# Loading, casting and turning the first two x pairs by row tile in a QKV projection, and casting the second w block by slices

## The chip, the core and the metric

The kernel runs on one core of a Trainium2 chip. The metric is the device time of one execution in microseconds (us); several executions are taken and their median is given. The program's engines are TensorE (PE for its matmuls, PEld for its weight loads), VectorE (DVE), ScalarE (ACT) and GpSimd (POOL); SyncE (SP) issues most of the DMAs, and its instructions run in program order like those of the others.

## The reference

`x` has the shape 16 x 512 x 768, `w_qkv` 768 x 2304, both float32. The output is 3 x 16 x 512 x 768, float32.

```python
qkv = np.matmul(x, w_qkv)
q = qkv[..., :hidden]
k = qkv[..., hidden:2*hidden]
v = qkv[..., 2*hidden:]
return np.stack([q, k, v], axis=0).astype(np.float32)
```

So it is one matrix product of 8192 x 768 by 768 x 2304, whose result is stored in three parts.

## The kernel before, in words

The 8192 rows of x are worked through in 32 pairs `p` of two row tiles of 128 rows. The 2304 columns of w are split into four blocks of 512, named by `q` (left or right half) and `c` (first or second block of that half), and a remainder of 256 columns (`w_rem`). K = 768 is split into six slices `j` of 128. w is loaded in float32 and rounded on the chip: block (0, 0) into `b1[0]` and block (0, 1) into `bt`, both bf16.

From pair 2 on, a half's 2 x 2 blocks are multiplied with seven products in place of eight (a scheme of Strassen's kind). It needs sums and differences of blocks of w (`sum_w`, on DVE, L119) and of x (`sums_x`, `s`), which take the time in which w is still being loaded. Pairs 0 and 1 are therefore multiplied plainly: `block(q, c, w, groups)` (L433) goes over groups of k slices and row tiles, adds into one PSUM bank a row tile, and gives back a list of ACT copies from PSUM (`finish`, L441) that the caller places. Row tiles 0 to 3 are the two of pair 0 and the two of pair 1.

The order of all work is written out by hand (`tc.manual_schedule()`), so each engine runs its instructions in the order in which the program makes them. What stands at the start, L399 to L566, is this:

- DMA issues on SP: pair 0 of x as one DMA (`load_rows`, L161), pair 1 as another, six slices of w block (0, 0) of 256 KB each, two halves of block (0, 1) of 768 KB each (L92), the first two of eight parts of pair 2 (L137, `load_x_rows`), the remainder of w (`str`), the other six parts of pair 2, then the halves of block (1, 0).
- Each DMA has one of eight completion semaphores in turn, and SP issues a DMA only when the one eight places earlier has landed. The trace shows this: the ninth issue comes at 5.01 us, pair 0 having landed at 4.99.
- Pairs 0 and 1 are cast to bf16 (`cast_rows`, half a row tile on DVE, L165, half on ACT, L167), turned by PE transposes (L187), six a row tile, and copied out of PSUM by the same two lines (`turn_rows`).
- PE first runs dummy matmuls on a tile of zeros (`busy`, L418), 11 ahead of the first transposes and 4 between the pairs.
- The slices of block (0, 0) are cast by DVE (`cast_k`, L429). `block(0, 0)` is 24 matmuls of 512 columns (L449). Its order, `singles`, gives pair 0 the first two slices ahead of pair 1.
- The halves of block (0, 1) are cast whole, the first by DVE (L426), the second by ACT (L424). Then come `sum_w(0, 1)` and `sum_w(0, 2)` on DVE, a cast of a half into `b22[0]` on POOL (L502), the four copies out of PSUM of block (0, 0) on ACT, and the casts of the remainder, half on DVE (L505), half on ACT (L506).
- `block(0, 1)` is another 24 matmuls; `rem(0)` and `rem(1)` are 24 of 256 columns (L303).
- Pair 2 is turned by DVE in two steps (`transpose(2, 2)`, L153): the first step needs parts 0 to 3 of its load, the second parts 4 to 7. A part is 96 KB and writes 32 of the 128 partitions. ACT then rounds row tile 0 (`round_row`, L204), copies `rems[0]` out (L317), copies two banks (L441), rounds row tile 1, copies `rems[1]`, and evacuates pair 2's product 1 (`evacuate`, L257).
- PE goes on with pair 2's products 1 and 2 (`do`, L248), its remainder (`rem(2)`, whose second half needs row tile 1), and product 6, which adds into the bank that `evacuate` reads, so it has to come after that.

From there on, products of pair 2 alternate with the plain blocks of the right half, and then the loop over the pairs runs.

Of the kernel before, what the change touches and what calls it, by code (L numbers as in the profile page):

```python
# [10 lines left out]
def kernel(  # L11
# [20 lines left out]
    nc = tc.nc  # L32
    P = 128
# [15 lines left out]
    bf16 = mybir.dt.bfloat16  # L49
    ident = mybir.ActivationFunctionType.Identity  # L50
# [3 lines left out]
    x_flat = x.rearrange("b t h -> (b t) h")  # L54
# [5 lines left out]
    tq_pool = ctx.enter_context(tc.tile_pool(name="tq", bufs=2))  # L60
# [14 lines left out]
    eye = w_pool.tile([P, 176], bf16, name="eye")[:, :P]  # L75
    w_rem = [w_pool.tile([P, KH, REM], bf16, name="w_rem0"), None]

    b1 = [w_pool.tile([P, KT, CB], bf16, name=f"b1_{q}") for q in range(2)]
# [6 lines left out]
    bt = both[:, 1].bitcast(bf16).rearrange("p (j n) -> p j n", j=KT)  # L85
# [4 lines left out]
    def load_w(dst, j0, nj, off, cols):  # L90
        rows = w_qkv.rearrange("(p j) n -> p j n", j=KT)
        nc.sync.dma_start(dst, rows[:, j0:j0 + nj, off:off + cols])  # L92

    stage = {}

    def load_blocks(q, c, nj=KH):
        if q == 0:
            t = tq_pool.tile([P, KT, CB], fp32, name="st0", tag="tq")
            for j in range(0, KT, nj):
                load_w(t[:, j:j + nj], j, nj, Q_OFF[q] + c * CB, CB)  # L100
            stage[q, 0, c], stage[q, 1, c] = t[:, :KH, :], t[:, KH:, :]
        else:
            for h in range(2):
                if c == 0 and h == 0:
                    t = st_first
                else:
                    t = st_pool.tile([P, KH, CB], fp32, name="st1", tag="st")[:]
                load_w(t, h * KH, KH, Q_OFF[q] + c * CB, CB)
                stage[q, h, c] = t

    def sum_w(q, n):
        t1, t2, t3, t4 = ts[q]
        o, in0, in1 = {
            1: (t1, stage[q, 0, 1], stage[q, 0, 0]),
            2: (t2, stage[q, 1, 1], t1),
            3: (t3, stage[q, 1, 1], stage[q, 0, 1]),
            4: (t4, stage[q, 1, 0], t2),
        }[n]
        nc.vector.tensor_tensor(o, in0, in1, op=sub)  # L119

    xin, xf, xb, sr = {}, {}, {}, {}
# [8 lines left out]
    def load_x_rows(p, parts=range(8)):  # L130
        if p not in xin:
            xin[p] = xin_pool.tile([P, 2 * P // G, KC], fp32, name="xin")
        rows = x_flat[p * 2 * P:(p + 1) * 2 * P, :].rearrange("(g b) k -> b g k", b=G)
        for n in parts:
            r, i = divmod(n, 4)
            gs = slice(r * P // G, (r + 1) * P // G)
            nc.sync.dma_start(  # L137
                xin[p][i * G:(i + 1) * G, gs], rows[:, gs, i * KC:(i + 1) * KC]
            )
# [15 lines left out]

    def load_rows(p):
        xin[p] = xin_pool.tile([P, 2, K], fp32, name="xin")
        rows = x_flat[p * 2 * P:(p + 1) * 2 * P, :]  # L160
        nc.sync.dma_start(xin[p][:], rows.rearrange("(r m) k -> m r k", m=P))  # L161

    def copy_halves(dst, src, two):

        nc.vector.tensor_copy(out=dst[0], in_=src[0])  # L165
        if two:
            nc.scalar.activation(dst[1], src[1], ident)  # L167
        else:
            nc.vector.tensor_copy(out=dst[1], in_=src[1])

    xc = {}

    def cast_rows(p, two=True):
        src = xin.pop(p)
        xc[p] = s_pool.tile([P, 2, K], bf16, name="xc", tag="s")
        for r in range(2):
            halves = (slice(0, K // 2), slice(K // 2, K))
            copy_halves([xc[p][:, r, n] for n in halves], [src[:, r, n] for n in halves], two)

    def turn_rows(p, two=True):  # L180
        c = xc.pop(p)
        xb[p] = xb_pool.tile([P, KT, 2 * P], bf16, name="xb", tag="xb")
        for r in range(2):
            cols = c[:, r, :].rearrange("m (p j) -> m j p", j=KT)
            ps = ps_pool.tile([P, KT, P], bf16, name="ps")
            for j in range(KT):
                nc.tensor.transpose(ps[:, j, :], cols[:, j, :], eye)  # L187
            ks = (slice(0, KH), slice(KH, KT))
            copy_halves(
                [xb[p][:, n, r * P:(r + 1) * P] for n in ks], [ps[:, n, :] for n in ks], two  # L190
            )

    def round_x(p):
        xb[p] = xb_pool.tile([P, KT, 2 * P], bf16, name="xb", tag="xb")
# [2 lines left out]
    act, dve = nc.scalar, nc.vector  # L197
# [32 lines left out]
    def quad(p, q, pool=o_pool, tag="o"):  # L230
        u = Quad()
        u.p, u.q = p, q
        u.o = pool.tile([P, 2, 2 * CB], fp32, name="o", tag=tag)
        u.x = u.y = u.z = None
        return u
# [17 lines left out]
    def bank():  # L253
        return ps_pool.tile([P, CB], fp32, name="ps")
# [144 lines left out]
    ND = 2  # L399
    zero = xb_pool.tile([P, CB], bf16, name="zero", tag="xb")  # L400
    nc.vector.memset(zero[:], 0.0)  # L401
    load_rows(0)
    nc.scalar.activation(tiny[:], zero[:, :1], ident)
    make_identity(nc, eye)
    load_rows(1)
    load_blocks(0, 0, 1)
    load_blocks(0, 1)
    st_rem = o_pool.tile([P, KT, REM], fp32, name="str", tag="o")
    load_x_rows(2, range(2))
    load_w(st_rem[:], 0, KT, R_OFF, REM)  # L410
    load_x_rows(2, range(2, 8))
    load_blocks(1, 0)

    def busy(n):

        ps = bank()
        for _ in range(n):
            nc.tensor.matmul(ps[:], zero[:, :P], zero[:], start=True, stop=True)  # L418

    def cast(q, h, c, w, eng):  # L420

        dst = w[:, h * KH:(h + 1) * KH, :]
        if eng is act:
            eng.activation(dst, stage[q, h, c], ident)  # L424
        else:
            eng.tensor_copy(out=dst, in_=stage[q, h, c])  # L426

    def cast_k(j):
        dve.tensor_copy(out=b1[0][:, j, :], in_=stage[0, j // KH, 0][:, j % KH, :])  # L429

    quads = {}

    def block(q, c, w, groups, between={}):  # L433

        ps = {}
        late = []

        def finish(n):
            p, r = divmod(n, 2)
            u = quads[p, q]  # L440
            act.activation(u.o[:, r, c * CB:(c + 1) * CB], ps[n][:], ident)  # L441

        for i, (js, tiles) in enumerate(groups):
            for n in tiles:
                p, r = divmod(n, 2)
                if n not in ps:
                    ps[n] = bank()
                for j in js:
                    nc.tensor.matmul(  # L449
                        ps[n][:], xb[p][:, j, r * P:(r + 1) * P], w[:, j, :],  # L450
                        start=(j == 0), stop=(j == KT - 1), skip_group_check=True,
                    )
                if KT - 1 not in js:
                    continue
                if (p, q) not in quads:
                    quads[p, q] = quad(p, q)
                late.append(lambda n=n: finish(n))
            between.get(i, lambda: None)()
        return late

    def halves(tiles):
        return [(range(h * KH, (h + 1) * KH), tiles) for h in range(2)]
# [18 lines left out]
        round_x(p)  # L481
        sums_x(p)

    singles = [((0, ), (0, 1)), ((1, ), (0, 1)), ((0, 1), (2, 3))]
    singles += [((j, ), range(4)) for j in range(2, KT)]

    busy(11)
    cast_rows(0)
    turn_rows(0)
    busy(4)  # L490
    cast_rows(1)
    cast_k(0)
    cast_k(1)
    turn_rows(1)
    for j in range(2, KT):
        cast_k(j)
    late0 = block(0, 0, b1[0], singles)
    cast(0, 0, 1, bt, dve)
    cast(0, 1, 1, bt, act)
    sum_w(0, 1)  # L500
    sum_w(0, 2)
    nc.gpsimd.tensor_copy(out=b22[0][:], in_=stage[0, 1, 1])  # L502
    for f in late0:
        f()
    dve.tensor_copy(out=w_rem[0][:], in_=st_rem[:, :KH])  # L505
    act.activation(w_rem[1][:], st_rem[:, KH:], ident)  # L506
    late = block(0, 1, bt, halves(range(4)))
    rems = [rem(p) for p in range(2)]
    transpose(2, 2)

# [19 lines left out]
    sum_w(0, 3)  # L530
    sums[3](dve)
    sums[4](dve)

    def cast_j(q, c, w, j):
        act.activation(w[:, j, :], stage[q, j // KH, c][:, j % KH, :], ident)

    u = quad(2, 0)
    do(u, 1)
# [2 lines left out]
    rem2 = rem(2)  # L541
    middle(u)
    cast_j(1, 0, b1[1], 1)
    store2 = []

# [16 lines left out]
    late = block(1, 0, b1[1], slices, {0: rest, 3: end})  # L562
# [65 lines left out]
```

## Time and profile before

| what | value |
|---|---|
| median of 3 executions | 361.02 us (360.87 to 361.2) |
| the profiled execution, its own time | 361.09 us |
| its span, first to last instruction | 359.3 us |
| time around the span | 1.79 us |
| PE busy | 352.2 us, 98% of the span |
| DVE, ACT, POOL busy | 229.0, 186.6, 176.7 us |
| moved by DMA | 108.09 MB, 301 GB/s in the mean |

A line of the timeline reads: start, duration, engine, line of the kernel, operation, what is written and read, shapes, number of instructions merged into it, and in brackets the idle time of the engine just before it and what ended that. Times are counted from the start of the span. A group's duration goes from its first start to its last end, and as matmuls are pipelined, groups overlap. An arrow `<-` in the brackets names the one waited for. Weight loads run beside matmuls.

### The profile page before, as it was taken

The numbers are of one execution on the slowest core, as the hardware profiler recorded it, in microseconds if no ns is written. First come the engines' busy times: TensorE is split into PE (matmuls) and PEld (weight loads), VectorE is DVE, ScalarE is ACT, GpSimd is POOL, SyncE is SP. The second block draws the span as 40 slices with busy tenths as digits, with TensorE's granted clock in tenths as the row PEclk, the third lists the DMA queues.
The fourth block names the chain that finished last, engine by engine and source line by source line (L and its number), as shares of the span: only waits on it lengthen the run. The fifth ranks groups of instructions, "written<-read, shape, count | busy, mean of one in ns | idle before, by whom it ended". The sixth has DMA issues, their size and how long they took to land.

```text
span 359.3 us, 5225 instructions
## 1 busy us (share of the span) xinstructions
PE 352.2 (98%) x1748; PEld 251.8 (70%) x1779; DVE 229.0 (64%) x241; ACT 186.6 (52%) x316; POOL 176.7 (49%) x183
## 2 busy tenths in 40 slices
PE   8999999999999999999999999999999999999995
PEld 3465577777777777777777777777777777777764
DVE  3899776666566675566675556676556676556643
ACT  4489744545444545444445444445444445545443
POOL 0101766436665445665444665444665444665420
PEclk9999999999999999999999999999999999999999
DMA  7999999798999999899999899898999999999767
GB/s 298 359 361 337 317 359 386 234 345 305 277 315 305 291 285 281 288 307 310 292 287 280 290 297 328 282 288 278 293 291 318 294 296 272 281 298 323 290 238 260
DMA packets 81563, 108.09 MB, mean 301 GB/s; under 512 B 4993, under 2 KB 61569, under 8 KB 81537
## 3 DMA queue, kind: packets, MB, share of 16 engines
q1 hardware_dynamic: 67216, 97.14, 82.9%
q10 hardware_dynamic: 14320, 10.62, 9.0%
q8 instruction: 14, 0.23, 0.3%
q14 instruction: 13, 0.10, 0.1%
HBM read 32.24 MB, written 75.50 MB: 300 GB/s over the span
## 4 chain that ended last, share of the span: by engine, by line
PE 97%; ACT 1%; issue 1%; ACTq 0%; DVE 0%
PE ps L248 78%; PE ps L303 11%; PE ps L449 6%; PE ps L418 1%; PE ps L187 1%; ACT o L283 0%; ACTq L358 0%; ACT orem L372 0%; ACT xb L167 0%; ACT xc L167 0%; ACTq L374 0%; DVE xb L165 0%; DVE zero L401 0%; ACTq L372 0%
## 5 line engine op out<-in xcount | busy, mean ns | idle before, releaser
L248 PE MATMUL ps<-t,s 128*128 128x512 f32 x720 | 181.2, 399 | 0.0
L248 PEld LDWEIGHTS ps<-t,s 128*128 128x128 f32 x720 | 135.0, 188 | 30.8
L195 POOL CAST xb<-xf 128x1536 bf16<-128x1536 f32 x28 | 41.0, 1464 | 131.6 <-DVE xf L153 131.6
L280 DVE TENSOR_TENSOR o<-o,ps 128x512 f32<-128x512 f32 x58 | 39.9, 688 | 91.2 <-ACT o L279 91.2
L153 DVE STREAM_TRANSPOSE xf<-xin 128x1536 f32<-128x1536 f32 (+1 forms) x32 | 88.7, 2774 | 1.3 <-DMA xin<-in_x_dram 1.2
L248 PE MATMUL ps<-b,xb 128*128 128x512 bf16 x331 | 85.1, 380 | 1.5
L248 PEld LDWEIGHTS <-xb 128*128 128x128 bf16 x360 | 32.8, 98 | 37.3 <-issue 7.6
L273 ACT ACTIVATE o<-ps 128x512 f32<-128x512 f32 x60 | 36.0, 600 | 44.1 <-PE ps L248 41.4
L279 ACT ACTIVATE o<-ps 128x512 f32<-128x512 f32 x58 | 34.7, 598 | 44.2 <-PE ps L248 44.2
L286 DVE TENSOR_TENSOR o<-o,ps 128x512 f32<-128x512 f32 x60 | 41.2, 687 | 21.4 <-PE ps L248 20.2
L248 PE MATMUL ps<-b,s 128*128 128x512 f32 x180 | 50.4, 389 | 0.0
L283 ACT ACTIVATE o<-ps 128x512 f32<-128x512 f32 x60 | 35.9, 598 | 24.5 <-PE ps L248 21.6
L257 ACT ACTIVATE o<-ps 128x512 f32<-128x512 f32 x60 | 35.9, 598 | 24.4 <-DVE o L286 20.7
L303 PE MATMUL ps<-w_rem,xb 128*128 128x256 bf16 x384 | 47.4, 273 | 0.0
L303 PEld LDWEIGHTS <-xb 128*128 128x128 bf16 x384 | 37.3, 98 | 11.5 <-issue 0.8
L270 DVE TENSOR_TENSOR o<-o,ps 128x512 f32<-128x512 f32 x60 | 37.8, 672 | 2.0 <-ACT o L257 1.3
L248 PEld LDWEIGHTS ps<-b,s 128*128 128x128 f32 x180 | 33.8, 188 | 7.1
L215 POOL TENSOR_TENSOR s<-xf 128x384 fp32r<-128x384 f32 x29 | 30.9, 1065 | 0.0
L216 POOL TENSOR_TENSOR s<-s,xf 128x384 fp32r<-128x384 f32 x29 | 29.5, 1016 | 2.3
L217 POOL TENSOR_TENSOR s<-xf 128x384 fp32r<-128x384 f32 x29 | 29.5, 1017 | 0.0
L219 POOL TENSOR_TENSOR s<-xf,s 128x384 fp32r<-128x384 f32 x29 | 29.5, 1017 | 0.0
L317 ACT ACTIVATE orem<-ps 128x512 f32<-128x512 f32 x31 | 18.5, 597 | 19.6 <-PE ps L303 19.6
(45 smaller groups left out, 119.5 us busy)
## 6 DMA issues: line engine op xcount, KB each, us to landing
out_dram<-o SPq DMA_DIRECT2D x62, 768.0 KB, 5.2
out_dram<-o SPq DMA_DIRECT2D x65, 256.0 KB, 4.1
xin<-in_x_dram SPq DMA_DIRECT2D x62, 192.0 KB, 6.9
xin<-in_x_dram ACTq DMA_DIRECT2D x50, 192.0 KB, 4.4
out_dram<-orem SPq DMA_DIRECT2D x31, 256.0 KB, 5.8
st<-in_w_qkv_dram SPq DMA_DIRECT2D x5, 768.0 KB, 8.0
xin<-in_x_dram SPq DMA_DIRECT2D x2, 768.0 KB, 5.0
st<-in_w_qkv_dram SPq DMA_DIRECT2D x6, 256.0 KB, 6.0
```

Of the source, the lines that this page charges most:

```text
L153: nc.vector.transpose(turned[:, g:g + n], rows[:, g:g + n])
L195: nc.gpsimd.tensor_copy(out=xb[p][:], in_=xf[p][:])
L215: 1: lambda g: g.tensor_tensor(s[:, 1], a21, a22, op=add),
L248: nc.tensor.matmul(ps[:], lhs[j], rhs[j], start=(start and j == 0), stop=(j == KH - 1), skip_group_check=True,)
L257: nc.scalar.activation(u.o[:, 0, :CB], u.x[:], ident)
L270: nc.vector.tensor_tensor(c11, c11, u.z[:], op=add)
L273: nc.scalar.activation(c12, u.x[:], ident)
L279: nc.scalar.activation(c22, u.x[:], ident)
L280: nc.vector.tensor_tensor(c22, c22, u.y[:], op=add)
L283: nc.scalar.activation(c21, u.x[:], ident)
L286: nc.vector.tensor_tensor(c12, c12, u.y[:], op=add)
L303: nc.tensor.matmul(ps, xb[p][:, j, r * P:(r + 1) * P], w_rem[j // KH][:, j % KH, :], start=(j == 0), stop=(j == KT - 1), skip_group_check= ...
```

## The change

Each row tile of pairs 0 and 1 gets a DMA, a cast and a turn of its own. Three row tiles are loaded ahead of w's first block, the fourth ahead of that block's last slice. The dummy matmuls go from 11 and 4 to 8, 2 and 1. Block (0, 0) takes row tiles 0 to 2 slice by slice, and row tile 3, turned ahead of the last slice, comes last with all six slices. The second w block is cast by slices on DVE and ACT instead of by halves, with the PSUM copies of block (0, 0) between them; its product takes the first half by slices. Only one part of pair 2 is loaded ahead of the remainder of w instead of two. The second half of the remainder is cast by POOL instead of ACT, ahead of the cast into `b22[0]`, and `b22[0]` thus waits for the remainder's landing. The bytes that are moved and the products are the same.

```diff
-    def load_rows(p):
...
-        nc.sync.dma_start(xin[p][:], rows.rearrange("(r m) k -> m r k", m=P))
+    def load_row(p, r):
...
+        nc.sync.dma_start(xin[p][:, r], x_flat[row:row + P, :])
...
-    load_rows(0)
+    load_row(0, 0)
     nc.scalar.activation(tiny[:], zero[:, :1], ident)
     make_identity(nc, eye)
-    load_rows(1)
-    load_blocks(0, 0, 1)
+    load_row(0, 1)
+    load_row(1, 0)
+    load_first(range(KT - 1))
+    load_row(1, 1)
+    load_first((KT - 1, ))
     load_blocks(0, 1)
+    load_x_rows(2, (0, ))
     st_rem = o_pool.tile([P, KT, REM], fp32, name="str", tag="o")
-    load_x_rows(2, range(2))
     load_w(st_rem[:], 0, KT, R_OFF, REM)
-    load_x_rows(2, range(2, 8))
+    load_x_rows(2, range(1, 8))
     load_blocks(1, 0)
...
-    singles = [((0, ), (0, 1)), ((1, ), (0, 1)), ((0, 1), (2, 3))]
-    singles += [((j, ), range(4)) for j in range(2, KT)]
-
-    busy(11)
-    cast_rows(0)
-    turn_rows(0)
-    busy(4)
-    cast_rows(1)
-    cast_k(0)
-    cast_k(1)
-    turn_rows(1)
-    for j in range(2, KT):
-        cast_k(j)
-    late0 = block(0, 0, b1[0], singles)
-    cast(0, 0, 1, bt, dve)
-    cast(0, 1, 1, bt, act)
+    three = [((j, ), range(3)) for j in range(KT)] + [(range(KT), (3, ))]
+
+    busy(8)
+    cast_row(0, 0)
+    turn_row(0, 0)
+    busy(2)
+    cast_row(0, 1)
+    cast_row(1, 0)
+    turn_row(0, 1)
+    busy(1)
+    cast_j(0, 0, b1[0], 0, dve)
+    turn_row(1, 0)
+    for j in range(1, KT - 1):
+        cast_j(0, 0, b1[0], j, dve)
+    cast_row(1, 1)
+    cast_j(0, 0, b1[0], KT - 1, dve)
+    late0 = block(0, 0, b1[0], three, {KT - 2: lambda: turn_row(1, 1)})
+    cast_j(0, 1, bt, 0, dve)
+    late0[0]()
+    late0[1]()
+    cast_j(0, 1, bt, 1, act)
+    cast_j(0, 1, bt, 2, dve)
+    late0[2]()
+    late0[3]()
     sum_w(0, 1)
+    cast_j(0, 1, bt, 3, dve)
+    cast_j(0, 1, bt, 4, act)
+    cast_j(0, 1, bt, 5, act)
     sum_w(0, 2)
+    dve.tensor_copy(out=w_rem[0][:], in_=st_rem[:, :KH])
+    nc.gpsimd.tensor_copy(out=w_rem[1][:], in_=st_rem[:, KH:])
     nc.gpsimd.tensor_copy(out=b22[0][:], in_=stage[0, 1, 1])
-    for f in late0:
-        f()
-    dve.tensor_copy(out=w_rem[0][:], in_=st_rem[:, :KH])
-    act.activation(w_rem[1][:], st_rem[:, KH:], ident)
-    late = block(0, 1, bt, halves(range(4)))
+    late = block(
+        0, 1, bt, [((j, ), range(4)) for j in range(KH)] + [(range(KH, KT), range(4))]
+    )
     rems = [rem(p) for p in range(2)]
     transpose(2, 2)
```

`cast_row` and `turn_row` hold the bodies of the loops over `r` of `cast_rows` and `turn_rows`; `cast_j` casts one k slice of a w block on ACT or DVE; `load_first` allocates the stage tile of block (0, 0) and loads the slices asked for. All that follows `transpose(2, 2)` is as before.

More of the change, by code (lines that the diff above doesn't have):

```diff
@@ L94, with load_first, load_blocks @@
     stage = {}
-    def load_blocks(q, c, nj=KH):
+    def load_first(js):
+        if (0, 0, 0) not in stage:
+            t = tq_pool.tile([P, KT, CB], fp32, name="st0", tag="tq")
+            stage[0, 0, 0], stage[0, 1, 0] = t[:, :KH, :], t[:, KH:, :]
+        for j in js:
+            load_w(stage[0, j // KH, 0][:, j % KH:j % KH + 1, :], j, 1, Q_OFF[0], CB)
+    def load_blocks(q, c):
         if q == 0:
             t = tq_pool.tile([P, KT, CB], fp32, name="st0", tag="tq")
-            for j in range(0, KT, nj):
-                load_w(t[:, j:j + nj], j, nj, Q_OFF[q] + c * CB, CB)
+            for j in range(0, KT, KH):
+                load_w(t[:, j:j + KH], j, KH, Q_OFF[q] + c * CB, CB)
             stage[q, 0, c], stage[q, 1, c] = t[:, :KH, :], t[:, KH:, :]
@@ L154, in transpose, with copy_halves @@
         xf[p] = t
-    def load_rows(p):
-        xin[p] = xin_pool.tile([P, 2, K], fp32, name="xin")
-        rows = x_flat[p * 2 * P:(p + 1) * 2 * P, :]
-        nc.sync.dma_start(xin[p][:], rows.rearrange("(r m) k -> m r k", m=P))
-    def copy_halves(dst, src, two):
+    def load_row(p, r):
+        if r == 0:
+            xin[p] = xin_pool.tile([P, 2, K], fp32, name="xin")
+        row = (2 * p + r) * P
+        nc.sync.dma_start(xin[p][:, r], x_flat[row:row + P, :])
+    def copy_halves(dst, src):
@@ L165, in copy_halves @@
         nc.vector.tensor_copy(out=dst[0], in_=src[0])
[L166 to L169, printed above, removed]
+        nc.scalar.activation(dst[1], src[1], ident)
     xc = {}
[L173 to L191, printed above, removed]
+    def cast_row(p, r):
+        if r == 0:
+            xc[p] = s_pool.tile([P, 2, K], bf16, name="xc", tag="s")
+        halves = (slice(0, K // 2), slice(K // 2, K))
+        copy_halves([xc[p][:, r, n] for n in halves], [xin[p][:, r, n] for n in halves])
@@ L193, in round_x, with turn_row @@
+    def turn_row(p, r):
+        if r == 0:
+            xb[p] = xb_pool.tile([P, KT, 2 * P], bf16, name="xb", tag="xb")
+        cols = xc[p][:, r, :].rearrange("m (p j) -> m j p", j=KT)
+        ps = ps_pool.tile([P, KT, P], bf16, name="ps")
+        for j in range(KT):
+            nc.tensor.transpose(ps[:, j, :], cols[:, j, :], eye)
+        ks = (slice(0, KH), slice(KH, KT))
+        copy_halves([xb[p][:, n, r * P:(r + 1) * P] for n in ks], [ps[:, n, :] for n in ks])
     def round_x(p):
@@ L418, in busy, with cast_j @@
             nc.tensor.matmul(ps[:], zero[:, :P], zero[:], start=True, stop=True)
-    def cast(q, h, c, w, eng):
-        dst = w[:, h * KH:(h + 1) * KH, :]
+    def cast_j(q, c, w, j, eng=act):
+        src = stage[q, j // KH, c][:, j % KH, :]
         if eng is act:
-            eng.activation(dst, stage[q, h, c], ident)
+            eng.activation(w[:, j, :], src, ident)
         else:
-            eng.tensor_copy(out=dst, in_=stage[q, h, c])
-    def cast_k(j):
-        dve.tensor_copy(out=b1[0][:, j, :], in_=stage[0, j // KH, 0][:, j % KH, :])
+            eng.tensor_copy(out=w[:, j, :], in_=src)
     quads = {}
@@ L532 @@
     sums[4](dve)
-    def cast_j(q, c, w, j):
-        act.activation(w[:, j, :], stage[q, j // KH, c][:, j % KH, :], ident)
     u = quad(2, 0)
```

## The prediction

> **What bounds the kernel now.** First the totals and the chain that ended last, on the page:
>
> ```profile
> PE 352.2 (98%) x1748; PEld 251.8 (70%) x1779; DVE 229.0 (64%) x241; ACT 186.6 (52%) x316; POOL 176.7 (49%) x183
> ...
> PE 97%; ACT 1%; issue 1%; ACTq 0%; DVE 0%
> ```
>
> PE is the bound nearly everywhere, so a gain at the start reaches the end only if PE stays ahead at every later wait. I therefore read PE's timeline over the first 26 us, where the change lies:
>
> ```profile
> 1.19 4.87 PE L418 MATMUL ps<-zero 128*128 128x512 bf16 x11 [1.19 <-DVE zero L401]
> 5.85 1.44 PE L187 MATMUL ps<-eye,xc 128*128 128x128 bf16 x12
> 7.12 1.03 PE L418 MATMUL ps<-zero 128*128 128x512 bf16 x4
> 8.67 0.95 PE L187 MATMUL ps<-eye,xc 128*128 128x128 bf16 x12 [0.52 <-ACT xc L167]
> 9.46 5.34 PE L449 MATMUL ps<-b,xb 128*128 128x512 bf16 x23
> 14.64 5.34 PE L449 MATMUL ps<-both,xb 128*128 128x512 bf16 x24
> 19.82 2.78 PE L303 MATMUL ps<-w_rem,xb 128*128 128x256 bf16 x24
> 22.66 1.24 PE L248 MATMUL ps<-b,xb 128*128 128x512 bf16 x5
> 23.74 1.47 PE L303 MATMUL ps<-w_rem,xb 128*128 128x256 bf16 x12
> 25.03 1.66 PE L248 MATMUL ps<-t,s 128*128 128x512 f32 x6
> ```
>
> PE idles once (0.52 us) and starts the first real matmul at 9.46. From there the groups follow without a gap. At 25.03 comes pair 2's product 6, which has to follow ACT's `evacuate` (L257). So ACT's timeline is next:
>
> ```profile
> 20.97 0.84 ACT L204 ACTIVATE xb<-xf 128x768 bf16<-128x768 f32 x1 [0.78 <-DVE xf L153]
> 21.72 0.58 ACT L317 ACTIVATE orem<-ps 128x512 f32<-128x512 f32 x1
> 22.20 1.08 ACT L441 ACTIVATE o<-ps 128x512 f32<-128x512 f32 x2
> 23.15 0.85 ACT L204 ACTIVATE xb<-xf 128x768 bf16<-128x768 f32 x1
> 23.88 0.61 ACT L317 ACTIVATE orem<-ps 128x512 f32<-128x512 f32 x1
> 24.36 0.62 ACT L257 ACTIVATE o<-ps 128x512 f32<-128x512 f32 x1
> ```
>
> ACT waits for DVE's transpose of pair 2, then runs six steps back to back until 24.98, and PE arrives at 25.03: ACT and PE meet there, with no slack on either side. What DVE waited for:
>
> ```profile
> 18.37 0.56 DVE L505 CAST w_rem<-str 128x768 bf16<-128x768 f32 x1
> 19.37 3.25 DVE L153 STREAM_TRANSPOSE xf<-xin 128x768 f32<-128x768 f32 x2 [0.44 <-DMA xin<-in_x_dram]
> ```
>
> DVE was free at 18.93 and waited 0.44 us for part 3 of pair 2, which the trace lands at 19.25. **A second chain thus ends at 25.03**: landing of part 3, transpose, six ACT steps, product 6. The change shortens PE's own way to 25.03, and touches the other chain only through the order of DMAs and POOL's casts.
>
> **Part by part.**
>
> *Arrival of x and w.* In the trace pair 0 (768 KB) lands at 4.99 and pair 1 at 6.89, 1.90 us later; a row tile is half, 0.95. The w slices land at 7.53, 8.22, 8.86, 9.46, 10.11 and 10.81, the halves of block (0, 1) at 12.72 and 14.95. With the new order I estimate row tiles at 4.04, 5.0 and 5.95, the first five slices 0.95 earlier (6.6 to 9.15), row tile 3 at 10.1, the last slice at 10.8 as before. SP has two more DMAs at about 0.45 us each (the two pairs' issues take 0.95 together). The ninth and tenth now wait for row tiles 0 and 1, and are issued at about 5.05 for bytes that move after 9.1: hidden.
>
> *PE until block (0, 0).* Dummies start every 0.43 us at first (eleven in 4.66) and 12 transposes take 1.27, 0.106 each; later they take 0.79, and a block matmul (14.64 - 9.46) / 24 = 0.216. Eight dummies end at 4.6. Row tile 0's casts (DVE 0.36, ACT 0.52) end at 4.58: six transposes until 5.3, two dummies until 6.15. The copies from PSUM start some 0.25 after the last transpose's start slot, and in the trace ACT's (0.49) starts only after DVE's (0.36) in all four pairs, so ACT ends row tile 0's at 6.4 and casts row tile 1 until 6.85. PE idles some 0.7 us there. Transposes, one dummy, transposes of row tile 2 until 7.9; casts of slices at 0.42 on DVE let block (0, 0) start at 8.3 instead of 9.46. Three matmuls a slice (0.65) keep step with the slices (0.64). Six more transposes (0.35) lie inside the block, and 24 matmuls take 5.2: it ends at 13.85, against 14.64. **PE's lead is 0.8 us**, or 0.3 if row tile 3's copies hold up the last slice by half a microsecond.
>
> *Block (0, 1).* Its first slice is cast on DVE from 12.74 (landing 12.72) to 13.2, ahead of 13.85. ACT's copies and casts (about 0.5 and 0.62 a step) reach slice 1 at 14, needed at 14.7, and slices 4 and 5 at 16.2, needed at 16.7. So the lead stays: end at 19.05 against 19.82.
>
> *The remainder.* It lands at 18.35 after two parts. With one part moved behind it I estimate 17.85, since 0.50 us lie between the landings of parts 0 and 1 (15.56 and 16.06). DVE's half is cast by 18.45. POOL's half has no row here. The nearest is POOL's 768-element cast at 37.67: 2.20 us, of which it did its work only after DVE's L119 ended at 39.18, so 0.70 alone. From both sides 0.70 to 2.20; I take 0.56 (behind DVE's cast) + 0.70, so ready at 19.15, and the fourth remainder matmul wants it at 19.4. Even at the upper end it is ready at 20.1, and PE still reaches pair 2 by 22.4, no later than before. ACT loses a cast of 0.84 at 18.37, which ended in idle time, so that is worth nothing.
>
> *Pair 2.* The same bytes come ahead of part 3 as before: parts 0 to 3 and the remainder. DMA is slower while these parts run, in the table of stretches (from, to; busy us of PE, PEld, DVE, ACT, POOL; clock, DMA share, GB/s):
>
> ```profile
> 17.50:18.75 1.25, 1.25 (x8) 0.54 (x7) 1.19 (x2) 1.25 (x3) 0.00 (x0) 1.00 1.14 211
> ...
> 21.00:22.25 1.25, 1.25 (x14) 1.12 (x13) 1.22 (x1) 1.25 (x3) 0.00 (x0) 1.00 1.05 398
> ```
>
> 211 against 398 GB/s. Parts in a row land 0.38 to 0.50 us apart. The remainder takes 2.29 us behind two parts; 768 KB at the 398 GB/s of the other row would be 1.98. Behind one part I take half of that excess away, 0.15, and round the saving in part 3's landing to **0.2 us** (19.05). Its ends: 0.2 later (one part's spread of spacing, doubled), and 1.0 earlier if all four parts went at 398 GB/s (0.25 each instead of 0.40 to 0.61), of which PE's lead lets 0.8 through. [...]
>
> So the chain moves by 0.2: ACT ends `evacuate` at 24.78. PE, with its lead of 0.8, waits for row tile 0 of pair 2 (21.65) and ends `rem(2)` by 24.5, then waits for `evacuate`. **Of 0.8 us of lead, 0.2 remain at product 6.** Later waits have room: product 7's sum is written by 25.73 and read at 27.22, t4 by 28.93 and read at 31.21. Block (1, 0)'s first half is now issued at 17.9 instead of 16.07, because its place in the ring waits for the remainder. The first packet ever came 1.0 us after its issue (0.74, 1.75), so its bytes stand ready when the parts end at about 20. Without that cover it still has 0.94 us between landing (23.90) and its cast (24.84).
>
> *Sum.* 361.09 - 0.2 = 360.9 for the profiled execution, whose own time is 0.07 over the median of the runs shown; from the median, 361.02 - 0.2 = **360.8**.
>
> **Rivals.**
>
> *The slow start of PE lasts longer.* Dummies went at 0.43 us until 7.1 and at 0.22 after. The granted clock reads 1.00 in every stretch of the profile, so only this pace shows it. PE had been busy without a break for 5.9 us by then; now it idles some 0.7 us ahead of that point. If the change of pace needs another 5.9 us of unbroken work, it comes at 6.85 + 5.9 = 12.75; at best it comes at 7.1 as before. In the middle, at 10, the 2.1 us from 7.9 on would do half their work and cost 1.05, so that the lead of 0.8 becomes a lag of 0.25: **361.3**; at the late end it costs 2.4 and the lag is 1.6 (362.6). For it: the pace changed only after unbroken work. Against: the gap of 0.52 at 8.15 did not bring the slow pace back. [...]
>
> *The parts land early.* At the upper end, 0.8 us: **360.2**. For it: 211 GB/s leave room. Against: the bytes ahead of part 3 don't change.
>
> *POOL holds DVE (slower).* `b22[0]`'s cast moves from 15.00 to about 19.15, beside DVE's transposes. Where both met in the trace, one waited: L119 at 15.41 took 2.90 beside POOL's L502, 1.75 alone. If a transpose waits so, the price is POOL's cast, 1.47, less the time that remains until part 3 lands: it decides as soon as `b22[0]` still runs when part 3 is there (19.15 + 1.47 = 20.6 against 19.05). Transpose and product 6 then move by 1.2 us net: **362.2**. Against: L119 reads two tiles in SBUF. L270, with one input in SBUF and one in PSUM, keeps 0.68 beside POOL's cast at 58.43, and POOL keeps its 1.46; a transpose has one input.
>
> **How the numbers follow.** Forecast 0.58, 360.8, own range 360.4 to 361.2; slow pace 0.17; early parts 0.13; POOL 0.12. The range takes in the first three, but for the late end of the slow pace, and stops short of the last: 360.2 to 361.8, 0.84 in all. About 0.2%, 0.7 us, is what a measurement here can tell from no change. Faster by that (under 360.3): most of the early parts, 0.11. Slower (over 361.7): POOL's case and the late end of the slow pace, 0.04, together 0.16. The rest, 0.73, is the same.
>
> **What would show it.** Right: L449 starts near 8.3 and block (0, 1) ends near 19; PE idles ahead of pair 2's product 1 and again ahead of product 6, waiting for ACT; DVE's first transpose starts near 19.2. Wrong: the transposes start below 18.8 or last over 1.6 us each; dummies and matmuls at 0.43 us after 8; PE without a wait between 21 and 25, which would mean that the second chain is not the bound.

## The result, and the profile after

The changed kernel takes **363.11 us** in the median (361.97 to 363.77, nine executions) where the kernel before takes 361.20 beside it (360.87 to 361.48, nine): a ratio of 1.0046, 95% interval 1.0031 to 1.0061 (ratios are of the means of the executions, so they can differ a little from those of the medians). It is slower, by about twice what the prediction called measurable, and outside its range. The profiled execution took 362.42 us with a span of 360.3, so 1.0 of its 1.33 us over the profile before lies in the span. The rest lies around the span (2.1 against 1.8 us). Other executions of the kernel before also have 1.8 to 2.1 there, so nothing is read from it. One execution each of two kernels below, `e_khalf` and `e_allload`, was disturbed (941 and 520 us); they are left out of the ratios, and of their profiles only the first 8 us of `e_khalf` are used.

First the totals and the chain on the page of the kernel after:

```profile
PE 353.1 (98%) x1775; PEld 250.3 (69%) x1775; DVE 229.4 (64%) x243; ACT 185.7 (52%) x317; POOL 177.4 (49%) x184
...
PE 91%; DMA 4%; ACT 2%; SPq 1%; DVE 0%; ACTq 0%; issue 0%
```

PE is still the bound, but the chain that ended last now runs through DMAs for 4% of the span, counted from issue to landing; before, DMA had no share in it. Two DMAs make up that share: the third w slice (issued at 3.07, landed at 9.03) and part 3 of pair 2 (12.40 to 20.14). From part 3 the chain goes through DVE's transpose and six ACT steps to product 6. PE's timeline of the kernel after shows what this did:

```profile
6.40 0.54 PE L189 MATMUL ps<-eye,xc 128*128 128x128 bf16 x6 [0.95 <-ACT xc L173]
...
7.48 0.54 PE L189 MATMUL ps<-eye,xc 128*128 128x128 bf16 x6 [0.32 <-ACT xc L173]
8.24 3.40 PE L448 MATMUL ps<-b,xb 128*128 128x512 bf16 x15 [0.22 <-DVE b L428]
...
12.41 2.10 PE L448 MATMUL ps<-b,xb 128*128 128x512 bf16 x9
14.35 5.48 PE L448 MATMUL ps<-both,xb 128*128 128x512 bf16 x24
19.67 2.94 PE L303 MATMUL ps<-w_rem,xb 128*128 128x256 bf16 x24
22.70 1.47 PE L248 MATMUL ps<-b,xb 128*128 128x512 bf16 x6
...
25.86 1.65 PE L248 MATMUL ps<-t,s 128*128 128x512 f32 x6
```

Block (0, 0) starts 1.22 us earlier than before (8.24 against 9.46). Block (0, 1) starts only 0.29 earlier, the remainder 0.15, pair 2's product 1 0.04 later, and product 6 **0.83 later** (25.86 against 25.03). That lag stays: the last matmul of the kernel starts 0.84 later than before. What holds product 6 up is the chain the prediction followed, here on ACT's timeline after and then on DVE's:

```profile
21.80 0.84 ACT L204 ACTIVATE xb<-xf 128x768 bf16<-128x768 f32 x1 [2.62 <-DVE xf L160]
...
25.18 0.62 ACT L257 ACTIVATE o<-ps 128x512 f32<-128x512 f32 x1
```

```profile
20.16 3.19 DVE L160 STREAM_TRANSPOSE xf<-xin 128x768 f32<-128x768 f32 x2 [0.74 <-DMA xin<-in_x_dram]
```

`evacuate` (L257) ends at 25.80 and product 6 follows. DVE waited 0.74 us for part 3 of pair 2, which the trace lands at 20.14 (19.25 before). From part 3 to product 6 nothing has become slower: the transposes take 1.60 and 1.57 us (1.56 and 1.58 before), the six ACT steps 4.0 as before. So the question is why part 3 is 0.89 late, with the same bytes ahead of it. The landings of both traces, from the start of the span:

| landing, us | before | forecast | after |
|---|---|---|---|
| first row tile or pair 0 | 4.99 (pair) | 4.04 | 3.88 |
| row tile 1 | | 5.0 | 4.92 |
| row tile 2 | 6.89 (pair 1) | 5.95 | **6.87** |
| first w slice | 7.53 | 6.6 | 7.73 |
| row tile 3 | | 10.1 | 11.26 |
| last w slice | 10.81 | 10.8 | **11.91** |
| halves of block (0, 1) | 12.72, 14.95 | | 13.83, 16.29 |
| part 0, remainder | 15.56, 18.35 | remainder 17.85 | 16.76, 18.84 |
| part 3 | 19.25 | 19.05 | **20.14** |

The first two row tiles are as forecast; the third comes 0.92 late, and nothing behind it makes this good: against the forecast, the first w slice is 1.13 late, the last 1.11 and part 3 1.09. The stretches of a microsecond (from, to; busy us of PE, PEld, DVE, ACT, POOL; clock, DMA share, GB/s) show where the bytes went. Before, then after:

```profile
4.00:5.00 1.00, 1.00 (x4) 0.30 (x2) 0.00 (x0) 0.00 (x0) 0.00 (x0) 1.00 1.04 415
5.00:6.00 1.00, 1.00 (x5) 0.42 (x4) 0.63 (x2) 0.94 (x2) 0.00 (x0) 1.00 1.01 412
6.00:7.00 1.00, 1.00 (x12) 1.00 (x11) 0.26 (x1) 0.00 (x0) 0.00 (x0) 1.00 1.02 396
```

```profile
4.00:5.00 1.00, 1.00 (x9) 0.48 (x8) 0.26 (x1) 0.42 (x1) 0.00 (x0) 1.00 1.09 243
5.00:6.00 1.00, 0.45 (x3) 0.00 (x0) 0.62 (x2) 0.55 (x2) 0.00 (x0) 1.00 0.90 283
6.00:7.00 1.00, 0.60 (x7) 0.42 (x7) 0.10 (x1) 0.45 (x2) 0.00 (x0) 1.00 0.94 301
```

The DMA engines count as busy nearly all the time in both (shares of 0.90 to 1.09 after), but move 827 KB instead of 1223. The 396 KB that are missing would take 0.96 us at 412 GB/s. The records of the packets say the same: x's packets of 3072 bytes take 121 ns in the median between 2 and 9 us, but eight of those that started at 4.1 to 4.4 took 528 to 1478 ns. In the trace before, none on that queue takes over 500 ns between 2.1 and 39 us. An instruction fetch in between isn't what did it: no trace of this case has one between 0.2 and 19 us.

### The profile page after: what moved, and what is told of

It is laid out like the page before. It is cut to its first block, busy times and chain, and to the rows that moved or that the text cites. A ratio compares the mean times of both kernels' runs of the same rounds, so it can differ in the third digit from the quotient of the medians.

```text
span 360.3 us, 5254 instructions
## 1 busy us (share of the span) xinstructions
PE 353.1 (98%) x1775; PEld 250.3 (69%) x1775; DVE 229.4 (64%) x243; ACT 185.7 (52%) x317; POOL 177.4 (49%) x184
## 4 chain that ended last, share of the span: by engine, by line
PE 91%; DMA 4%; ACT 2%; SPq 1%; DVE 0%; ACTq 0%; issue 0%
PE ps L248 78%; PE ps L303 10%; PE ps L448 3%; DMA xin<-in_x_dram 2%; DMA st<-in_w_qkv_dram 2%; SPq L144 1%; DVE xf L160 0%; ACT xb L204 0%; SPq L92 0%; SPq L169 0%; ACT o L283 0%; ACTq L358 0%; ACT o L440 0%; ACT orem L317 0%; ACT orem L372 0%
## 5 line engine op out<-in xcount | busy, mean ns | idle before, releaser
L248 PE MATMUL ps<-b,xb 128*128 128x512 bf16 x360 | 87.7, 380 | 0.1
L257 ACT ACTIVATE o<-ps 128x512 f32<-128x512 f32 x60 | 35.9, 598 | 24.3 <-DVE o L286 20.6
```

The source lines that it names most:

```text
L248: nc.tensor.matmul(ps[:], lhs[j], rhs[j], start=(start and j == 0), stop=(j == KH - 1), skip_group_check=True,)
L257: nc.scalar.activation(u.o[:, 0, :CB], u.x[:], ident)
```

## The experiments

Three theories were put to the test. **Arrival**: x loaded in small DMAs at the start stalls the DMA engines, everything behind comes about 1 us late, and the chain of part 3 carries it to the end. **Clock**: PE's idle time before 8.5 us costs it the granted clock (the prediction's first rival). **POOL**: the casts moved to POOL hold DVE (its last rival). Ratios are to the kernel before on the same chip, with 95% intervals.

### The change again, x in pairs again, and more dummies

`c_after` is the changed kernel once more.

> The changed kernel unchanged, for a second profile and more times. Theory A (the DMA stream slows when row tile 2 begins, 4 to 7 us, and the loss is carried through part 3, the transpose and ACT to product 6): the profile again shows under 300 GB/s between 4 and 6 us and row tile 2 landing near 6.9, product 6 near 25.9, median 362 to 363.5. Theory B (PE's slow pace lasts longer in some executions): the DMA stream is at 400 GB/s in some profiles, and the executions with a lower mean granted clock are the long ones. Theory C (one chance stall in the one profile): row tile 2 lands near 5.95, product 6 near 25, and the time is long for a reason not seen yet.

Measured: 362.53 against 361.22 us, ratio 1.0041 (1.0026 to 1.0057). Its profile shows the same with a larger lag: row tile 2 at 7.43, part 3 at 20.84, product 6 at 26.55. Here a single DMA engine makes the lag: 15 of the 16 had delivered row tile 2 by 5.94, as forecast, and part 3 by 19.34; the landings at 7.43 and 20.84 are those of the sixteenth. So the loss varies between executions, and so does the time (361.6 us for the profiled span here, 360.3 in the first).

`e_pairload` is the changed kernel with both pairs of x loaded as before, ahead of w:

```diff
-    load_row(0, 0)
+    load_rows(0)
...
-    load_row(0, 1)
-    load_row(1, 0)
-    load_first(range(KT - 1))
-    load_row(1, 1)
-    load_first((KT - 1, ))
+    load_rows(1)
+    load_first(range(KT))
```

> The changed kernel with pairs 0 and 1 of x loaded by one DMA each, both ahead of w, as before; all computing as in the change. Theory A, if the splitting or the new order is what slows the stream: x lands at 4.99 and 6.89, the last w slice near 10.8, part 3 near 19.1, median 360.7 to 361.3. Theory B: the dummies are still fewer and PE still idles, so it stays at 362 to 363.5.

Measured: 362.12, ratio 1.0029 (1.0017 to 1.0041). The profiled execution (span 359.3) has no long packets between 2.3 and 19 us: the pairs land at 5.00 and 6.85, the last slice at 10.77, the remainder at 17.71 and part 3 at 18.93. Product 6 on its PE timeline:

```profile
24.74 1.66 PE L247 MATMUL ps<-t,s 128*128 128x512 f32 x6
```

It is 0.29 *earlier* than before. So with x in pairs the forecast holds in the profiled execution, which speaks for the arrival theory. But the executions are still slower in the median (spans of 359.3 to 361.6), and the profiled one gives its lead back between 79 and 86 us, where x comes late (last matmul at 355.30 against 355.24 before). The intervals of the two ratios, with and without the split, overlap. The arrival isn't all of it.

`e_busy` is the changed kernel with `busy(6)` and `busy(3)` in place of `busy(2)` and `busy(1)`, which keeps PE working through the waits.

> The changed kernel with 6 and 3 dummy matmuls in place of 2 and 1, so that PE has hardly a gap ahead of block (0, 0). Theory A: unchanged, 362 to 363.5, part 3 as late as without. Theory B: the long executions go away, 361 to 362, and the granted clock is near 1.0 in all.

Measured: 362.42, ratio 1.0033 (1.0022 to 1.0045). On its PE timeline the waits before block (0, 0) are gone but for 0.12 us, and product 6 is as late as in the changed kernel:

```profile
4.95 1.46 PE L421 MATMUL ps<-zero 128*128 128x512 bf16 x6
...
8.14 3.41 PE L448 MATMUL ps<-b,xb 128*128 128x512 bf16 x15
...
25.82 1.66 PE L248 MATMUL ps<-t,s 128*128 128x512 f32 x6
```

Part 3 lands at 20.11. A PE that hardly idled didn't help while part 3 was late.

### The small loads alone, in the kernel before

`e_split4` is the kernel before with x of pairs 0 and 1 in four DMAs of a row tile, all ahead of w. Nothing else changes.

```diff
-        nc.sync.dma_start(xin[p][:], rows.rearrange("(r m) k -> m r k", m=P))
+        nc.sync.dma_start(xin[p][:, r], x_flat[row:row + P, :])
```

> The kernel before with its two x loads split into four row tile DMAs, all ahead of w; nothing else changed. Theory A, if the split alone slows the stream: under 300 GB/s for a microsecond or two between 4 and 7, part 3 near 20, and 0.5 to 1.0 over the kernel before. If the order (w behind three row tiles) is needed for it: within 0.2 of the kernel before. Theory B: within 0.2.

Measured: 363.55, ratio **1.0070** (1.0057 to 1.0083): this one edit costs more than the whole change, and more than either theory gave it. Row tiles 0 to 2 land at 3.88, 4.95 and 5.88, but row tile 3 at 7.39, the last slice at 11.28 and part 3 at 19.81, and product 6 starts at 25.50, 0.47 late; packets took up to 986 ns at 5.2. The stretches of its profile:

```profile
4.00:5.00 1.00, 1.00 (x4) 0.37 (x3) 0.30 (x2) 0.46 (x2) 0.00 (x0) 1.00 1.02 402
5.00:6.00 1.00, 1.00 (x15) 0.88 (x14) 0.56 (x2) 0.49 (x1) 0.00 (x0) 1.00 0.94 249
```

One stretch at 249 GB/s; the one after it has 390. The profiled execution took 361.78 and is the shortest of six (the others 363.3 to 364.4), so even this understates the loss. Six further kernels ask what it is about these loads. `e_split0` splits pair 0 alone:

> The kernel before with pair 0 of x alone loaded by two row tile DMAs, pair 1 by one. If any early small x DMA brings the stalls: packets over 600 ns between 3.4 and 6 and 0.5 to 2 over before. If it takes four of them, or the later ones: a stream of 400 GB/s from 3 on and within 0.3 of before.

Measured: 364.20, ratio 1.0059 (1.0036 to 1.0081). Pair 1, one whole DMA again, lands at **8.41** instead of 6.89: 15 engines had delivered by 7.27, one was over a microsecond behind, while the rate between 4 and 7 us was 362 to 375 GB/s. Part 3 came at 22.40, product 6 at 28.18 (3.15 late), and PE's timeline has waits for x, for block (0, 1) and for the remainder:

```profile
9.01 0.95 PE L191 MATMUL ps<-eye,xc 128*128 128x128 bf16 x12 [1.43 <-ACT xc L171]
...
18.53 2.75 PE L453 MATMUL ps<-both,xb 128*128 128x512 bf16 x12 [0.51 <-ACT both L428]
21.96 2.79 PE L307 MATMUL ps<-w_rem,xb 128*128 128x256 bf16 x24 [0.68 <-DVE w_rem L509]
```

`e_khalf` cuts each pair by columns instead of rows, so its packets are 1536 bytes:

> The kernel before with each pair's x load split into two DMAs by columns, so that each reads both row tiles in packets of 1536 bytes: as many DMAs of the same size as e_split4, other addresses. If the count or size of the DMAs slows the stream: as e_split4, 2 over before, with slow packets near 4 to 6. If reading one stretch of 384 KB a DMA slows it: no slow packets, part 3 near 19.3 to 19.6, within 0.4 of before.

Measured: ratio 1.0059 (1.0036 to 1.0082). In the first 8 us of its only, disturbed, profile the records show packets of 768 to 1085 ns at 5.0 to 5.7; on that execution this is weak evidence. `e_swap` is `e_split0` with row tile 1 loaded first, so that DVE and ACT, which start with row tile 0, read no x before 5.3 us:

> As e_split0, with the second row tile of pair 0 loaded first, so that the first cast starts when the second DMA lands, near 4.9 as before, and not at 3.9. If DVE, ACT and PE starting a microsecond earlier is what disturbs the stream: no packets over 600 ns between 3 and 7, pair 1 near 6.9 and 361 to 361.5. If the small early DMAs do it, whoever reads them: stalls as in e_split0, 362 to 364.5.

Measured: 362.67, ratio 1.0053 (1.0030 to 1.0075), longest packets of 826 to 1194 ns at 4.1 to 5.6, pair 1 at 9.26. Two of them started before 5.3, so the stall doesn't need an early reader. `e_late0` loads pair 1 whole first and then pair 0 in two; `e_order` does that without the split:

> As e_split0, with pair 1 loaded first in one DMA and then pair 0 in two row tiles. The first landing is near 5.0 as before, so the ninth issue on SP waits as before, but the two small DMAs are still there. Pair 0 comes 1.9 later, so the time is 1.5 to 2 over before in any case; what counts is the stream. If a first landing before 4 (and the issues that follow it) is what matters: no stalls. If the size of the x DMAs matters: packets over 600 ns as the row tiles or the slices behind them move, between 5 and 8.

> The kernel before with pair 1 of x loaded ahead of pair 0, both in one DMA each: e_late0 without its split. Pair 0 comes 1.9 later, so 1 to 2 over before in any case. If the split is what brings the stalls: no packets over 800 ns before 7, the first landing near 5.0. If it is what is read first: stalls of about 1 us near 2 to 3.4 as in e_late0, first landing near 5.9.

Measured: ratios 1.0057 (1.0040 to 1.0074) and 1.0039 (1.0024 to 1.0055). Both start with packets of about 1000 ns at 1.9. So this order brings slow packets with whole loads too. Only `e_late0`, with the split, stalls a second time (up to 993 ns at 2.9 to 3.3); `e_order` runs at 393, 412 and 406 GB/s from 3 to 6 us. The order of the pairs isn't what that second stall needs. Last, `e_count` is `e_split0` with the last two w slices in one DMA, so that there are as many early DMAs as before:

> As e_split0 (pair 0 in two row tile DMAs), with the last two slices of w block (0, 0) in one DMA, so that the number of early DMAs is that of the kernel before. If the number of DMAs brings the stalls: none, pair 1 near 6.9, within 0.5 of before. If it is the small x DMAs at the start: stalls between 3.4 and 6, 0.5 to 3 over.

Measured: 364.20, ratio 1.0074 (1.0049 to 1.0099). The stretches of its profile:

```profile
4.00:5.00 1.00, 1.00 (x3) 0.30 (x2) 0.23 (x1) 0.39 (x1) 0.00 (x0) 1.00 0.93 267
5.00:6.00 1.00, 1.00 (x5) 0.45 (x4) 0.36 (x1) 0.52 (x1) 0.00 (x0) 1.00 0.76 301
```

The number of DMAs isn't it either. What holds in every profile: in each kernel that splits an early x load (the change, `c_after`, `e_busy`, `e_split4`, `e_split0`, `e_khalf`, `e_swap`, `e_late0`, `e_count`) the longest packet between 2.5 and 6 us takes 826 to 1478 ns. In the nine profiles with whole pairs that can be used none takes over 615. Of the first nine, the profile of `e_khalf` is the disturbed one. Why remains open.

### The load order and the compute order, each alone

`e_allload` is the changed kernel's compute with all loads in the order of the kernel before; `e_alternate` is that with pair 2's parts in another order, so that consecutive parts write different halves of the partitions:

```diff
-    load_x_rows(2, range(2))
+    load_x_rows(2, (0, 2))
...
-    load_x_rows(2, range(2, 8))
+    load_x_rows(2, (1, 3, 4, 6, 5, 7))
```

> The changed kernel with the whole order of loads of before: pairs of x in one DMA each, two parts of pair 2 ahead of the remainder. Only the computing is changed. Theory A (the loads cost the time; computing is worth nothing because the second chain binds): product 6 at 24.9 to 25.1, median within 0.3 of the kernel before. Theory B (the computing, with fewer dummies or the POOL casts, costs part of it): 0.5 or more over before although part 3 lands near 19.25.

> As e_allload, but the parts of pair 2 in the order 0, 2 before the remainder and 1, 3, 4, 6, 5, 7 after it, so that neighbours in the queue write the two halves of the partitions in turn. If DMA is slow there because neighbours write the same half, the parts run faster, the first four are there 0.3 to 0.6 earlier than in e_allload and, with PE's lead, product 6 and the median move by the same. If the parts are slow for their size of 768 bytes, nothing moves.

Measured: 362.10, ratio 1.0022 (1.0013 to 1.0031), and 361.95, ratio 1.0016 (1.0008 to 1.0025). In the profile of `e_alternate` (span 359.0) the parts land 0.28 to 0.35 us apart, the last of parts 0 to 3 at 18.13, and DVE's first transpose starts 1.12 earlier than before; from 14 to 17 us the loads run at 371 to 378 GB/s (before 316, 231 and 381). On its DVE and PE timelines:

```profile
18.25 3.06 DVE L160 STREAM_TRANSPOSE xf<-xin 128x768 f32<-128x768 f32 x2 [0.17 <-DMA xin<-in_x_dram]
```

```profile
24.77 1.63 PE L247 MATMUL ps<-t,s 128*128 128x512 f32 x6
```

With part 3 over a microsecond early, product 6 still comes only 0.26 earlier: now PE's own work is the bound, and the changed order of compute has given it no more than that. So the compute order is worth at most 0.3 us here, and the median is slower all the same: 8 of its 11 executions have spans of 359.7 to 360.0. Why the parts went faster in this order is not shown.

The reverse, `e_onepart`, is the kernel before with only one part of pair 2 ahead of the remainder, and nothing else of the change:

```diff
-    load_x_rows(2, range(2))
+    load_x_rows(2, range(1))
...
-    load_x_rows(2, range(2, 8))
+    load_x_rows(2, range(1, 8))
```

> The kernel before with one part of pair 2 instead of two ahead of the remainder; nothing else changed. My forecast of this edit: the remainder lands near 17.85 instead of 18.35, part 3 near 19.05, time within 0.2 of before since PE has no lead. Rival: the next w block's issue, which now waits for the remainder, makes later loads late, so 0.2 to 1.0 over before, with later transposes waiting for their x.

Measured: **360.85** against 361.18, ratio 0.9990 (0.9981 to 0.9999). On ACT's timeline `evacuate` starts at 23.79 (24.36 before), and on PE's product 6 at 24.76:

```profile
23.79 0.62 ACT L257 ACTIVATE o<-ps 128x512 f32<-128x512 f32 x1
```

```profile
9.26 5.34 PE L449 MATMUL ps<-b,xb 128*128 128x512 bf16 x23
...
24.76 1.64 PE L248 MATMUL ps<-t,s 128*128 128x512 f32 x6
```

The remainder lands at 17.29 and part 3 at 18.56, 0.69 earlier than before, and ACT is done 0.35 ahead of PE. But 0.20 of PE's 0.27 stand already at block (0, 0), where the order of the loads can't have put them (PE's fast pace came at 6.68 in this execution, at 7.11 in the profile before). This is the best of all versions, by a tenth of a per cent. `e_best`, which adds the alternating order of parts to it, is the same:

> The kernel before with one part of pair 2 ahead of the remainder (as e_onepart) and the other parts in the order 2, 1, 3, 4, 6, 5, 7, so that neighbours write different halves of the partitions. PE has little lead in the kernel before, so at most 0.3 better than e_onepart's 0.3: 360.5 to 360.9. If only PE's own way counts: the same as e_onepart.

Measured: 361.00, ratio 0.9991 (0.9982 to 0.9999), product 6 at 24.76.

### The clock, and POOL

`e_nopool` is `e_alternate` with the remainder's second half cast by ACT again, so that the cast into `b22[0]` doesn't wait for it:

```diff
-    nc.gpsimd.tensor_copy(out=w_rem[1][:], in_=st_rem[:, KH:])
+    act.activation(w_rem[1][:], st_rem[:, KH:], ident)
```

> As e_alternate, with the second half of the remainder cast by ACT again and the cast into b22 no longer behind it on POOL. If POOL's casts cost the long executions: one group of spans near 358.9. If PE's gaps do: two groups as in e_alternate, median near 361.9.

Measured: 361.91, ratio 1.0016 (1.0007 to 1.0024), as `e_alternate`: POOL isn't the cause of the long executions. Its profile shows what the others hadn't. The stretches, with the granted clock behind the engines, and PE's timeline:

```profile
4.50:7.80 3.30, 1.45 (x14) 0.76 (x14) 1.34 (x4) 1.76 (x4) 0.00 (x0) 1.00 1.03 403
7.90:11.30 3.40, 3.40 (x16) 1.66 (x15) 2.79 (x9) 1.40 (x3) 0.00 (x0) 0.50 1.05 406
```

```profile
8.96 4.56 PE L444 MATMUL ps<-b,xb 128*128 128x512 bf16 x15
...
15.63 5.36 PE L444 MATMUL ps<-both,xb 128*128 128x512 bf16 x24
```

PE worked only 1.45 of 3.30 us up to 7.8, and then **had half the clock for 3.4 us**. Block (0, 0) takes 6.67 us instead of 5.2, and product 6 starts at 25.97, 0.94 later than before, though parts 0 to 3 of pair 2 had landed by 18.78. This execution's mean clock is 0.994. `e_allload` has 0.994 or 0.995 in five of its ten executions, `e_pairload` 0.994 in three of eleven, the changed kernel 0.993 in two of nine. The 105 executions of the kernel before beside these experiments all have 0.998 or more. `e_order`, which has all the dummies of before but gets pair 0 later, has 0.993 to 0.995 in three of ten. But of the eight long executions of `e_alternate` only one is under 0.998, so for the other seven this mean shows no lost clock.

`e_fill` keeps PE working instead: `e_alternate` with `busy(6)` and `busy(5)`.

> As e_alternate, with 6 and 5 dummy matmuls in place of 2 and 1, so that PE hardly idles ahead of block (0, 0). If PE's gaps cost e_alternate its long executions (spans of 359.7 to 360.0 in 8 of 11, 358.8 to 359.0 in 3): all spans under 359.2, median 361.0 or less. If POOL's casts or something else cost them: still two groups, median near 361.9.

Measured: 362.57, ratio 1.0047 (1.0028 to 1.0065), with six spans of 359.6 to 359.7 and six of 361.2 to 362.2. The first profile was one of the short ones. `e_fill_again` is the same kernel for another profile:

> e_fill unchanged, for another profile: 6 of its 12 executions had spans over 361. If this one is of those, a stall of one or more DMA engines before 7 us shows pair loads can meet it too; if it is of the short ones (359.6), this stays open.

It came out long, a span of 362.0, without a stall of the loads. On its PE timeline:

```profile
6.20 2.76 PE L417 MATMUL ps<-zero 128*128 128x512 bf16 x6
...
11.06 3.69 PE L444 MATMUL ps<-b,xb 128*128 128x512 bf16 x14
```

Its loads are on time (pairs at 4.96 and 6.88). Six dummies take 2.76 us where the short execution needs 1.46: the fast pace came only at 9.90, and block (0, 0) starts at 11.06 instead of 9.28. Both executions idle for the same 0.78 us ahead of 5.56; in the short one the fast pace had come at 4.89, before that gap. The mean clock didn't count this late start: it reads 0.999 here. These six, meant to save the clock, cost 1.30 us more where the fast pace came late. So neither forecast of `e_fill` holds, and what makes most of the executions of `e_alternate` long stays open.

## Why the prediction was wrong

**What bounds the kernel: right.** The second chain (part 3, transpose, six ACT steps, product 6) decides. In the changed kernel part 3 is 0.89 late and product 6 0.83, and in `e_pairload` part 3 is 0.32 early and product 6 0.29. Where part 3 comes earlier still (`e_onepart`, `e_alternate`), PE's own work is the bound.

**Arrival of x and w: this step failed.** It took a row tile as half of a pair, 0.95 us, so row tile 2 at 5.95 and the last slice still at 10.8. They landed at 6.87 and 11.91 (7.43 and 12.28 in `c_after`). That a split load moves its bytes at the pace of a whole one was taken for granted, and no rival was made of it. In the profiled execution this step accounts for the miss: part 3 is 1.09 behind its forecast of 19.05, and product 6 1.03 behind 24.83. `e_split4` shows that the split alone costs 0.57 to 0.83%.

**PE until block (0, 0): right in its result, by luck.** Start 8.24, forecast 8.3, with two errors that offset each other. Row tile 2 came 0.92 late, and the fast pace came at 4.27, not at 7.1 "at best". Of the lead of 0.8, 0.29 was left at block (0, 1), since the last nine matmuls of block (0, 0) start at 12.41, when the last slice is cast.

**Block (0, 1) and the remainder: right but for the arrival.** In the profile after, PE loses only 0.14 us in block (0, 1) and 0.19 in the remainder against before; in `c_after` and `e_busy` the remainder, which lands later there, holds PE up (0.71 + 0.19 and 0.18 + 0.19 us, on DVE's half and then on POOL's). POOL's cast took 1.21 us, 0.56 + 0.70 = 1.26 forecast.

**Pair 2: the mechanism right, the saving undersized.** One part moved behind the remainder was put at 0.2. In `e_onepart` part 3 lands 0.69 earlier, of which 0.16 stood at the second half of block (0, 1) already (14.79 against 14.95), so about 0.5. (The first packet of the profile before starts at 1.83, not at the 1.75 that the prediction reads; nothing hangs on it.) In the changed kernel it gives part of the lateness back: part 0 is 1.20 late, part 3 0.89.

**The sum.** Forecast -0.2 at product 6, measured +0.83 with +0.84 at the last matmul. The median is 2.3 us over the forecast of 360.8, so the 1.03 that the profile shows at product 6 is under half of the whole miss. For the executions that are longer still, the profiles of other executions and kernels show two possible sources: a larger stall (`c_after`, product 6 at 26.55) and the clock (`e_nopool`). How the nine executions of the changed kernel divide between them can't be told, since only one has a trace.

**The slow start of PE: underrated.** The argument against it, that a gap of 0.52 didn't bring the slow pace back, was too weak: in `e_nopool`, with gaps of 0.90 and 0.96, it did come back. In `e_alternate` it didn't, with gaps of 0.91 and 0.95, so the gap alone doesn't decide. Nor does the fast pace need 5.9 us of unbroken work, as the rival had it: in the profile after it came 3.1 us after PE's first dummy. The rival didn't act in the profile after, and `e_busy` shows that it isn't the main cause, but a slow pace kept the compute order from paying in `e_nopool` (+0.94 at product 6) and in `e_fill_again` (27.75 against 25.41 in the short execution, so 2.3).

**The parts land early: true of the parts, worthless here.** `e_alternate` has them 1.1 us early, and PE itself then limits the gain to 0.26.

**POOL holds DVE: wrong.** The cast into `b22[0]` ran at 20.05 to 21.51, beside the first transpose, which took 1.60 us against 1.56 in the kernel before. POOL's cast itself took 1.46.

## What to carry to other kernels

A load that is cut in pieces so that work can start sooner isn't paid by its first piece alone (here row tile 0 landed 1.11 us ahead of the pair it was cut from, and w's last slice 1.10 later than before): check when the *last* piece and all that is queued behind it land, and try the split by itself, in the old order of compute. Look for the next chain ahead of counting a lead: here 1.2 us at the start of a block became 0.3 at its end and a lag at the first meeting with another engine. And where dummy work is taken away, look at the granted clock of many executions: in the changed kernel it was 0.993 in two of nine and 0.998 or more in the others, so a single profile can't clear the change.

## What the hardware showed

- **The early split loads stalled.** Whole 768 KB loads ran at 393 to 421 GB/s from 3 to 8 us. With 384 KB pieces of the same bytes the change fell to 243 to 301 for 3 us, and the other kernels had a lowest microsecond of 227 to 275, but for `e_split0`, where one DMA engine lagged and the rate stayed at 362 or more from 3 to 7 us. Single packets took up to 1478 ns instead of 121. Early readers (`e_swap`), the order of the pairs (`e_order`) and the number of DMAs (`e_count`) were tried, with one profile each, and aren't the cause, which stays open.
- **Early in two profiles half the clock was granted for 3.4 us.** In the records it lasted from 7.88 to 11.30 in `e_nopool` and from 8.91 to 12.32 in `e_late0`; the stretches of 7.9 to 11.3 and 9.0 to 12.2 read 0.50, those ahead of them and behind them 1.00. PE was busy for some 45% and 41% of the 3.4 us before; with 49% in `e_alternate` (4.89 to 8.30) and 63% in the change (4.27 to 7.68) the clock stayed. It also stayed with some 45% in `e_swap` (6.75 to 10.16), so these runs don't show a share that decides. The first grant in the records came between 4.27 (the change) and 9.90 (`e_fill_again`).
- **Parts that alternated between the halves of the partitions landed closer together.** The last five parts of 96 KB landed 0.39 to 0.43 us apart in the mean when they came in order (the kernel before, `e_onepart`, `e_pairload`, `e_order`), and 0.33 to 0.37 when consecutive ones wrote different halves (`e_alternate`, `e_best`, `e_nopool`, `e_fill`, `e_fill_again`).
